# h held in SBUF through the first unit of a hybrid gMLP and Mamba-2 layer, and the gating norms' scalings moved off ScalarE

## The chip, the cores and the metric

One core of a Trainium2 chip. The metric is the device time of one execution in microseconds (us). The kernel before takes 1588.07 us, the median of three runs.

## The reference, cut to what matters

```python
def hybrid_layer(x, ...):                       # x: 2048 tokens of 1024 channels, float32
    h = rms_norm(x, pre_w)
    proj = einsum('bld,dc->blc', h, w_in)       # u, v, zg, z, xbc, dt_raw
    y_a = spatial_gating(u, v, zg, ...)
    y_b = ssd_mixer(xbc, z, dt_raw, ...)        # conv, SiLU, chunked scan, gated norm
    return x + rms_norm(concat(y_a, y_b) @ w_out, post_w)

def spatial_gating(u, v, zg, ...):
    vn = layer_norm(v, v_norm_w, v_norm_b)
    s = einsum('hts,bcshd->bcthd', tril(ws), vn) + bs    # within chunks of 128 tokens
    return grouped_rms_norm(u * s * silu(zg), out_norm_w, 128)
```

## The kernel before, in words

The tokens are four batches of 512 (b = 0 to 3), each of four chunks c of 128. The two projections run in seven **units** u: 0 and 2 make the channels xbc of two SSD groups each, 1 makes z, 3 makes v, 4 and 5 make u and zg for the gating, 6 is the output projection. A unit multiplies in Strassen-Winograd form: two pairs of batches p, (0, 2) and (1, 3), and seven products P1 to P7 over half the depth each (line 43). A **step** is one product's share of 256 in depth, `j`; a unit has 28 steps (two j), the last has 56 (four j). Each operand is split into a rounded part and its remainder (`split`, line 157: ScalarE copies, VectorE subtracts), and `mm3` (line 164, matmuls of lines 165 to 167) issues three matmuls of 128x512 for each of 2 x 4 combinations: 24 in a step. `after` (line 868) combines the products on VectorE.

The A operand of a step comes from h, the normed input, in layout [channels, tokens]. `prep(b)` (line 242) makes it: eight loads of half rows of x (256 KB each, into buffers of the `g` pool), their sums of squares on ScalarE (line 184), the inverse root on POOL, a diagonal matrix `dg` and a matmul with ones that spreads it over the partitions (`r_ps`, line 259), a copy `rb` (line 261). Then for each of four j a load of x_t (512 KB), the scaling of its two halves on VectorE (line 268), the store to the DRAM tensor `hd`, and the passes of the small dt projection on PE (line 273; the profile counts two passes for each matmul call, 64 a batch). After them comes `dt_chain` (line 286), whose cumulative sum `cs` is what the scan's decay is made from; it starts 20 time units after its batch's prep.

`make_a` (line 721) is a generator for one step: up to its `yield` it issues loads, behind it arithmetic. In unit 0 the plain products P1, P2 and P4 load one tile of `hd`, P6 loads three, P5 two, P3 one; P7 takes what P6 left. P6 subtracts twice, keeps `s3` and, by a POOL copy, `s2` for P7 and P3. Made operands of P6, P7, P5 and P3 are stored (`a_d`) and loaded by later units; unit 1 loads the plain ones from `hd` again. `look_ahead` (line 833) makes A two steps and B three steps ahead of the matmuls.

Work beside the products is in generators, too. `spawn(gen, delay)` sets one up, `yield d` asks to go on `d` time units later, and `run_tasks` lets at most a few go on after each group of six matmuls, which counts as 1.36 units (about 1 us each). `tc.issue_after` keeps what such a task puts on PE behind the matmuls already written. Stores are queued by `store` and issued 5.4 units later. All transfers are issued by SP. The framework's scheduler fixes the order on each engine from a timeline of its own, so a load that depends on nothing can be issued long before the line that asks for it.

In the gating, `spatial(b, hp)` (line 574) handles 256 channels: it loads v, normalizes it (line 584 on VectorE: minus the mean, times the weight; line 585 on ScalarE: times the inverse deviation r), multiplies with the masked matrix (line 594) and adds `SB`, the row bias (line 598, VectorE). `gate_in` (line 608) multiplies with u and SiLU(zg) when the projection's sums arrive, and `gate_out` (line 622) scales by the norm (line 627, ScalarE, eight operations of 128x128), waits 14 units and transposes (`y_tiles`, line 547). There are 16 such tiles of work in units 4 and 5; six of the eight of a unit come in its last 11 steps (`WANTED`, line 909). POOL also serves the SSD scan: lines 436, 438, 457, 464 and 465.

Buffers of a pool are shared by its tiles: `r` has 7 of 128x1024, `g` 32 of 128x515, `q` 22 of 128x256.

Of the kernel before, what the change touches and what calls it, by code (L numbers as in the profile page):

```python
# [15 lines left out]
P = 128  # L16
# [35 lines left out]
def hybrid_kernel(ctx: ExitStack, tc: tile.TileContext, x, x_t, pre_w, w_u, w_o, w_dt,  # L52
# [64 lines left out]

    def setup():
# [4 lines left out]
        nc.sync.dma_start(out=y_c[:, 8:16], in_=sn_w)  # L123
        nc.sync.dma_start(out=wsT, in_=ws_t)
# [18 lines left out]
    def row_weights(src):  # L143
        t = const.tile([P, DM], F32, name="row_w")
        nc.sync.dma_start(out=t, in_=src.partition_broadcast(P))
        return t
# [16 lines left out]

    def mm3(dst, a_hi, a_lo, b_hi, b_lo, first, last):
# [16 lines left out]
    junk = const.tile([P, WC], mybir.dt.bfloat16, name="junk")  # L181
# [53 lines left out]
    def load_x(b):  # L235
        for c in range(NT):
            for n in range(2):
                xt = gt("xt")
                nc.sync.dma_start(out=xt, in_=x[(b * NT + c) * P:(b * NT + c + 1) * P, n * WC:(n + 1) * WC])
                yield c, n, xt  # L240

    def prep(b):

        ss = sm.tile([P, NT, 2], F32, name="x_ss")
        dg = gt("dg").rearrange("p (c n) -> p c n", c=NT)
        for c, n, xt in load_x(b):
            sumsq(ss[:, c, n:n + 1], xt, WC)
        if b == 0:
            for i, v in enumerate((dt_bias, a_log, d_skip)):
                nc.sync.dma_start(out=hvec[:, i, :], in_=v.partition_broadcast(P))  # L250
            nc.scalar.activation(na, hvec[:, 1, :], AF.Exp)
            nc.vector.tensor_scalar(na, na, -1.0, None, ALU.mult)
        r = rsqrt_mean2(ss, NT, 1.0 / DM, "x")
# [9 lines left out]
        for j in range(4):  # L263
            h = rt("h")
            nc.sync.dma_start(out=h, in_=x_t[b, j])
            for kk in range(2):
                k = 2 * j + kk
                nc.vector.scalar_tensor_tensor(h[:, kk, :], h[:, kk, :], pre_c[:, k:k + 1], rb, ALU.mult, ALU.mult)
            nc.sync.dma_start(out=hd[b][j], in_=h)
            for kk in range(2):  # L270
                k = 2 * j + kk
                for c in range(NT):
                    nc.tensor.matmul(dtp[:, c * NH:(c + 1) * NH], lhsT=h[:, kk, c * P:(c + 1) * P], rhs=wdt[:, k, :],
                                     start=k == 0 and c == 0, stop=k == KT - 1 and c == NT - 1, skip_group_check=True)
            if b:
                yield 0
# [5 lines left out]
        spawn(dt_chain(b, d), 20)  # L282

# [437 lines left out]
    def make_a(u, p, name, j):  # L721
# [17 lines left out]
        if u == 0:  # L739
            yield  # L740
# [266 lines left out]
```

## Time and profile before

| | |
|---|---|
| median of three runs (lowest to highest) | 1588.07 us (1584.94 to 1588.9) |
| the profiled execution: its own time / its span | 1584.35 / 1582.6 us |
| granted TensorE clock, mean over the span | 0.979 |
| busy share of the span: PE, VectorE (DVE), ScalarE (ACT), POOL | 95%, 68%, 52%, 25% |
| moved by DMA | 494.63 MB, mean 313 GB/s |

How to read it: the span runs from the first to the last instruction of one profiled execution. PE is TensorE's matmul, PEld its weight load, SPq the sequencer that issues the transfers. A matmul's end is modelled and runs into the next one's start, so PE's busy time is more than the sum of what the matmuls need; the spacing of the starts is the better measure. A wait is put down to what came last before it ended. L12 is line 12 of the kernel.

### The profile page before, as it was taken

Reading aid. Unit: us, or ns where it says so; the run is one execution under the profiler, and the core shown is the slowest. Engines: PE = TensorE matmul, PEld = TensorE weight load, DVE = VectorE, ACT = ScalarE, POOL = GpSimd, SP = SyncE. Lnnn points to the kernel's source line nnn. Section 1 sums busy time; section 2 is a strip of 40 time slices with the busy share of each in tenths; the row PEclk is TensorE's granted clock in tenths of the full one; section 3 lists DMA queues with packets and bytes.
Section 4 is the critical chain, followed back from the end, with each engine's and each line's share of the span. In section 5 each row is a group of like instructions: output and inputs, shape, how many; then the busy total and the mean of one; then the engine's idle time right before and its main releaser. Section 6 shows DMA issues by size and latency. Waiting matters only on the chain.

```text
span 1582.6 us, 21521 instructions
## 1 busy us (share of the span) xinstructions
PE 1508.9 (95%) x7268; PEld 1258.4 (80%) x7268; DVE 1068.9 (68%) x1708; ACT 819.8 (52%) x1769; POOL 390.1 (25%) x449
## 2 busy tenths in 40 slices
PE   4979999899999999999999999989999999999996
PEld 3868887788888888888778888867888878888775
DVE  3476874678665576567786768764665646587698
ACT  4432324655676545654466666859737742333332
POOL 1000000234232333342234515353523300000022
PEclk9988999999999999999999999989999999999999
DMA  9799999999998799986998788866776598897998
GB/s 333 264 371 357 338 411 397 392 340 366 374 349 311 240 353 341 329 316 238 333 338 319 271 299 275 279 229 225 276 252 242 193 302 326 275 384 239 341 351 333
DMA packets 160847, 494.63 MB, mean 313 GB/s; under 512 B 19040, under 2 KB 35808, under 8 KB 140768
## 3 DMA queue, kind: packets, MB, share of 16 engines
q1 hardware_dynamic: 160736, 493.25, 85.9%
q8 instruction: 57, 0.93, 0.2%
q14 instruction: 54, 0.44, 0.1%
HBM read 373.51 MB, written 119.67 MB: 312 GB/s over the span
## 4 chain that ended last, share of the span: by engine, by line
PE 57%; DMA 13%; DVE 11%; ACT 7%; issue 3%; POOL 1%; SPq 1%; DVEq 0%; ACTq 0%; POOLq 0%
PE acc L165 16%; PE acc L167 16%; PE acc L166 16%; DMA E<-scr 3%; DMA r<-yd 3%; PE y_ps L448 3%; ACT E L389 2%; DMA r<-w_o 2%; PE y_ps L451 1%; PE st_ps L453 1%; DVE cv_out L372 1%; DVE a L161 1%; PE s_ps L594 1%; PE y_tp L553 1%; DVE b L161 1%
## 5 line engine op out<-in xcount | busy, mean ns | idle before, releaser
L165 PE MATMUL acc<-b,a 128*128 128x512 f32 x1344 | 544.6, 406 | 16.1 <-DMA a<-as0P 5.4
L166 PE MATMUL acc<-b,a 128*128 128x512 f32 x1344 | 527.3, 392 | 0.0
L167 PE MATMUL acc<-b,a 128*128 128x512 f32 x1344 | 520.2, 393 | 4.3 <-DVE a L161 4.3
L165 PEld LDWEIGHTS acc<-b,a 128*128 128x128 f32 x1344 | 253.7, 189 | 71.3 <-DMA a<-as0P 5.6
L167 PEld LDWEIGHTS acc<-b,a 128*128 128x128 f32 x1344 | 253.2, 188 | 60.2 <-DVE a L161 6.3
L166 PEld LDWEIGHTS acc<-b,a 128*128 128x128 f32 x1344 | 254.0, 189 | 49.3
L160 ACT ACTIVATE a<-r 128x1024 fp32r<-128x1024 f32 x96 | 101.1, 1057 | 200.8 <-PE acc L167 88.5
L165 PE MATMUL acc<-a,b 128*128 128x512 f32 x448 | 182.4, 414 | 8.3 <-ACT b L160 4.2
L372 DVE SCALAR_TENSOR_TENSOR cv_out<-cv_raw,cw,cv_out 128x512 f32<-128x512 f32 x192 | 155.1, 810 | 41.5 <-ACT cv_out L370 39.5
L161 DVE TENSOR_TENSOR b<-r,b 128x1024 fp32r<-128x1024 f32 x112 | 141.9, 1270 | 60.6 <-ACT b L160 60.4
L166 PE MATMUL acc<-a,b 128*128 128x512 f32 x448 | 180.3, 403 | 0.8 <-DVE a L161 0.8
L167 PE MATMUL acc<-a,b 128*128 128x512 f32 x448 | 177.7, 400 | 0.0
L160 ACT ACTIVATE b<-r 128x1024 fp32r<-128x1024 f32 x112 | 117.2, 1052 | 86.9 <-PE acc L167 33.1
L161 DVE TENSOR_TENSOR a<-r,a 128x1024 fp32r<-128x1024 f32 x96 | 117.3, 1223 | 50.5 <-ACT a L160 50.3
L165 PEld LDWEIGHTS acc<-a,b 128*128 128x128 f32 x448 | 87.2, 195 | 27.4 <-ACT b L160 4.3
L184 ACT ACTIVATE junk<-y 128x128 bf16<-128x128 f32 (+1 forms) x192 | 65.5, 341 | 83.1 <-POOL y L465 71.4
L457 POOL TENSOR_TENSOR state<-state,ex 128x256 f32<-128x256 f32 x60 | 46.9, 781 | 239.5 <-PE y_ps L451 239.4
L166 PEld LDWEIGHTS acc<-a,b 128*128 128x128 f32 x448 | 86.8, 194 | 19.6 <-DVE a L161 1.8
L167 PEld LDWEIGHTS acc<-a,b 128*128 128x128 f32 x448 | 86.4, 193 | 18.9 <-issue 0.2
L436 POOL TENSOR_TENSOR xde<-xtok,dte 128x256 f32<-128x256 f32 x64 | 52.3, 824 | 165.0 <-ACT xtok L408 158.7
L173 POOL TENSOR_TENSOR o_r<-o_ms,mhalf 128x1 f32<-128x1 f32 x16 | 19.0, 1198 | 295.1 <-DVE o_ms L171 285.0
L389 ACT ACTIVATE E<-E,cs 128x128 f32<-128x128 f32 x256 | 79.6, 390 | 22.2 <-DMA E<-scr 22.2
(163 smaller groups left out, 2125.8 us busy)
## 6 DMA issues: line engine op xcount, KB each, us to landing
a<-as0P SPq DMA_DIRECT2D x64, 1024.0 KB, 7.4
a<-as1P SPq DMA_DIRECT2D x64, 1024.0 KB, 6.2
r<-w_u SPq DMA_DIRECT2D x108, 512.0 KB, 6.4
r<-yd SPq DMA_DIRECT2D x72, 512.0 KB, 5.3
r<-hd SPq DMA_DIRECT2D x48, 512.0 KB, 7.5
r<-w_o SPq DMA_DIRECT2D x36, 512.0 KB, 5.2
E<-scr SPq DMA_DIRECT2D x64, 256.0 KB, 7.4
yd<-yT SPq DMA_DIRECT2D x64, 256.0 KB, 4.4
```

Source lines behind the costliest of these rows:

```text
L160: nc.scalar.activation(w[:, :, 0, :], t, AF.Copy)
L161: nc.vector.tensor_tensor(w[:, :, 1, :], t, w[:, :, 0, :], ALU.subtract)
L165: nc.tensor.matmul(dst, lhsT=a_hi, rhs=b_hi, start=first, stop=False, skip_group_check=True)
L166: nc.tensor.matmul(dst, lhsT=a_hi, rhs=b_lo, start=False, stop=False, skip_group_check=True)
L167: return nc.tensor.matmul(dst, lhsT=a_lo, rhs=b_hi, start=False, stop=last, skip_group_check=True)
L173: nc.gpsimd.tensor_tensor(r, ms, mhalf[:, 0:n], ALU.pow)
L184: nc.scalar.activation(junk[:, 0:n], src, AF.Square, accum_out=dst)
L372: nc.vector.scalar_tensor_tensor(cv, raw[:, j:j + T], cw[:, ti, j:j + 1], cv, ALU.mult, ALU.add)
L389: nc.scalar.activation(E[:, h, :], E[:, h, :], AF.Relu, scale=-1.0, bias=dts[self.b]["cs"][:, o + h:o + h + 1])
L436: nc.gpsimd.tensor_tensor(h4(xde[:, :]), xc, hv(d["dte"], g, c), ALU.mult)
L448: nc.tensor.matmul(yps[:, h * HD:(h + 1) * HD], lhsT=E[:, h, :], rhs=xdt[:, h * HD:(h + 1) * HD], start=True, stop=True)
L457: nc.gpsimd.tensor_tensor(h4(st[:, :]), h4(st[:, :]), ev(d["ex"], 1, g, c), ALU.mult)
```

## The change

- **prep** loads x as whole rows, four tiles of 512 KB in `r` buffers, and x_t as eight tiles of 256 KB in `g` buffers (`load_h`). Batches 0 and 1 issue both at once at the start; batch 2 is spawned after 2 units instead of 16, batch 3 after 10 instead of 30, and the waits between their parts are given as arguments. The sum of squares takes a whole row at a time. The scaled tiles stay in SBUF (`kept`), and are still stored to `hd`.
- **make_a in unit 0**: P1 and P2 take batch 0's and 1's tiles from `kept` (`take_h`, which runs the batch's prep on as far as needed) and split them in two halves (`split_tiles`). P6 loads one tile and takes batch 2's or 3's four from `kept`; it makes the sum for P5 there (`s1`), in four tiles of 128x256, and overwrites `a22` instead of copying it on POOL. P5 loads nothing; P3 and P4 load one tile as before.
- **look_ahead** makes the first two steps' A and B in turn.
- **held**: the loads of wsT, SB and the two row weights follow a one-column copy from batch 0's `cs`.
- **Gating**: v is normalized by one operation with two scalars; the weight is multiplied in on reading the matmul's result (VectorE), `SB` is added by POOL, and the norm's scaling is done by POOL in four operations of 128x256.

```diff
+    def held(t):
+        nc.vector.tensor_copy(t, dts[0]["cs"][:, 0:1])
...
+        held(wsT[:, 0, 0:1])
+        held(SB[:, 0, 0:1])
...
     def row_weights(src):
         t = const.tile([P, DM], F32, name="row_w")
+        held(t[:, 0:1])
         nc.sync.dma_start(out=t, in_=src.partition_broadcast(P))
         return t
...
+    def split_tiles(t):
+        w = apool.tile([P, 2, 2, T], F32R, name="a")
+        for kk in range(2):
+            n = T // len(t[kk])
+            for i, part in enumerate(t[kk]):
+                cols = slice(i * n, (i + 1) * n)
+                nc.scalar.activation(w[:, kk, 0, cols], part, AF.Copy)
+                nc.vector.tensor_tensor(w[:, kk, 1, cols], part, w[:, kk, 0, cols], ALU.subtract)
+        return w
...
+    kept, h_in = {}, set()
+    def prep(b, *waits):
+        xs = [rt("xt") for _ in range(NT)]
         for c in range(NT):
-            for n in range(2):
-                xt = gt("xt")
-                nc.sync.dma_start(out=xt, in_=x[(b * NT + c) * P:(b * NT + c + 1) * P, n * WC:(n + 1) * WC])
-                yield c, n, xt
-    def prep(b):
-        ss = sm.tile([P, NT, 2], F32, name="x_ss")
-        dg = gt("dg").rearrange("p (c n) -> p c n", c=NT)
-        for c, n, xt in load_x(b):
-            sumsq(ss[:, c, n:n + 1], xt, WC)
+            nc.sync.dma_start(out=xs[c], in_=x[(b * NT + c) * P:(b * NT + c + 1) * P, :]
+                              .rearrange("p (k t) -> p k t", k=2))
+        if b < 2:
+            hs = load_h(b)
         if b == 0:
             for i, v in enumerate((dt_bias, a_log, d_skip)):
                 nc.sync.dma_start(out=hvec[:, i, :], in_=v.partition_broadcast(P))
-            nc.scalar.activation(na, hvec[:, 1, :], AF.Exp)
-            nc.vector.tensor_scalar(na, na, -1.0, None, ALU.mult)
-        r = rsqrt_mean2(ss, NT, 1.0 / DM, "x")
+        else:
+            yield waits[0]
+        ss = sm.tile([P, NT], F32, name="x_ss")
+        for c in range(NT):
+            sumsq(ss[:, c:c + 1], xs[c][:, :, :].rearrange("p k t -> p (k t)"), DM)
+        del xs
+        r = sm.tile([P, NT], F32, name=f"x_r{b}", bufs=1)
+        nc.vector.tensor_scalar(r, ss, 1.0 / DM, EPS, ALU.mult, ALU.add)
+        nc.gpsimd.tensor_tensor(r, r, mhalf[:, 0:NT], ALU.pow)
+        if b:
+            yield waits[1]
+        if b > 1:
+            hs = load_h(b)
+            yield waits[2]
+        dg = gt("dg").rearrange("p (c n) -> p c n", c=NT)
...
-            h = rt("h")
-            nc.sync.dma_start(out=h, in_=x_t[b, j])
-            for kk in range(2):
-                k = 2 * j + kk
-                nc.vector.scalar_tensor_tensor(h[:, kk, :], h[:, kk, :], pre_c[:, k:k + 1], rb, ALU.mult, ALU.mult)
-            nc.sync.dma_start(out=hd[b][j], in_=h)
-            for kk in range(2):
-                k = 2 * j + kk
+            for k in (2 * j, 2 * j + 1):
+                nc.vector.scalar_tensor_tensor(hs[k], hs[k], pre_c[:, k:k + 1], rb, ALU.mult, ALU.mult)
+            if b < 2:
+                kept[b, j] = hs[2 * j:2 * j + 2]
+            yield 0
+            for k in (2 * j, 2 * j + 1):
+                nc.sync.dma_start(out=hd[b][j][:, k % 2, :], in_=hs[k])
+            h_in.add((b, j))
+            if b > 1:
+                kept[b, j] = hs[2 * j:2 * j + 2]
+            for k in (2 * j, 2 * j + 1):
                 for c in range(NT):
-                    nc.tensor.matmul(dtp[:, c * NH:(c + 1) * NH], lhsT=h[:, kk, c * P:(c + 1) * P], rhs=wdt[:, k, :],
+                    nc.tensor.matmul(dtp[:, c * NH:(c + 1) * NH], lhsT=hs[k][:, c * P:(c + 1) * P], rhs=wdt[:, k, :],
                                      start=k == 0 and c == 0, stop=k == KT - 1 and c == NT - 1, skip_group_check=True)
-            if b:
-                yield 0
+                hs[k] = None
+        if b == 0:
+            nc.scalar.activation(na, hvec[:, 1, :], AF.Exp)
+            nc.vector.tensor_scalar(na, na, -1.0, None, ALU.mult)
...
+    def load_h(b):
+        hs = [gt("h") for _ in range(KT)]
+        for k in range(KT):
+            nc.sync.dma_start(out=hs[k], in_=x_t[b, k // 2, :, k % 2, :])
+        return hs
+    def take_h(b, j):
+        while (b, j) not in kept:
+            advance(preps[b])
+        return kept.pop((b, j))
     dts = {}
...
-            nc.vector.scalar_tensor_tensor(vc, vc, mv[:, c, 0:1], row_w["v"][:, cols], ALU.subtract, ALU.mult)
-            nc.scalar.activation(vc, vc, AF.Copy, scale=r[:, c:c + 1])
+            nc.vector.tensor_scalar(vc, vc, mv[:, c, 0:1], r[:, c:c + 1], ALU.subtract, ALU.mult)
...
             for cc in range(2):
                 y = qt("y")
-                nc.vector.tensor_tensor(y, sps[:, cc * 256:(cc + 1) * 256],
-                                        SB[:, 2 * hp:2 * hp + 2, :].rearrange("p h d -> p (h d)"), ALU.add)
+                nc.vector.tensor_tensor(y, sps[:, cc * 256:(cc + 1) * 256], row_w["v"][:, cols], ALU.mult)
+                nc.gpsimd.tensor_tensor(y, y, SB[:, 2 * hp:2 * hp + 2, :].rearrange("p h d -> p (h d)"), ALU.add)
...
         r = rsqrt_mean(ss[:, :, :].rearrange("p c i -> p (c i)"), NT * 2, 1.0 / P, "g")
         for c in range(NT):
-            for i in range(2):
-                nc.scalar.activation(yg[c][:, i * P:(i + 1) * P], yg[c][:, i * P:(i + 1) * P], AF.Copy,
-                                     scale=r[:, 2 * c + i:2 * c + i + 1])
+            y = yg[c][:, :].rearrange("p (i d) -> p i d", i=2)
+            nc.gpsimd.tensor_tensor(y, y, r[:, 2 * c:2 * c + 2].unsqueeze(2).broadcast_to([P, 2, P]), ALU.mult)
         yield 14
         yield from y_tiles(b, yg, hp)
...
+            assert (b, 2 * k + j) in h_in
...
-    s2_in, s3_in = {}, {}
+    s1_in, s2_in, s3_in = {}, {}, {}
...
+        if u == 0 and name in ("P1", "P2"):
+            yield
+            b, k = PAIRS[p][0], PLAIN_A[name][1]
+            yield split_tiles([[h] for h in take_h(b, 2 * k + j)])
+            return
...
-        if u == 0:
-            yield
         if name == "P6":
             if u == 0:
-                t, q, r = load([piece(0, 0), piece(1, 0), piece(1, 1)])
-                tt(t, t, q, ALU.subtract)
-                s3_in[p, j] = t
-                tt(r, r, t, ALU.subtract)
-                s2 = s2_in[p, j] = [gt("s2") for _ in range(2)]
+                t, = load([piece(0, 0)])
+                yield
+                b = PAIRS[p][1]
+                a21, a22 = take_h(b, j), take_h(b, 2 + j)
+                s3_in[p, j], s2_in[p, j] = t, a22
+                s1 = s1_in[p, j] = [[], []]
                 for kk in range(2):
-                    nc.gpsimd.tensor_copy(s2[kk], r[:, kk, :])
-                t = r
+                    for cols in (slice(0, GC), slice(GC, T)):
+                        q = qt("s1")
+                        tt(q, a21[kk][:, cols], a22[kk][:, cols], ALU.add)
+                        s1[kk].append(q)
+                    tt(t[:, kk, :], t[:, kk, :], a21[kk], ALU.subtract)
+                    tt(a22[kk], a22[kk], t[:, kk, :], ALU.subtract)
+                w = split_tiles([[a] for a in a22])
+                store(a_d[p][name, j], w[:, :, :, :].bitcast(F32))
+                yield w
+                return
             else:
...
         elif name == "P7":
             if u == 0:
+                yield
                 t = s3_in.pop((p, j))
             else:
                 t, q = load([piece(0, 0), piece(1, 0)])
...
         elif name == "P5":
+            if u == 0:
+                yield
+                w = split_tiles(s1_in.pop((p, j)))
+                store(a_d[p][name, j], w[:, :, :, :].bitcast(F32))
+                yield w
+                return
             t, q = load([piece(1, 0), piece(1, 1)])
-            if u:
-                yield
+            yield
             tt(t, t, q, ALU.add)
         elif u == 0:
             t, = load([piece(0, 1)])
+            yield
             s2 = s2_in.pop((p, j))
             for kk in range(2):
                 tt(t[:, kk, :], t[:, kk, :], s2[kk], ALU.subtract)
...
         if i == 0:
             upto(0, 0, load_a)
             upto(1, 0, load_b)
+        for k in range(LOOK_A if i == 0 else 0):
+            upto(2, k, lambda *a: (load_a(*a) if looked[0] <= a[0] else None, do_a(*a),
+                                   looked.__setitem__(0, max(looked[0], a[0] + 1))))
+            upto(3, k, lambda *a: (load_b(*a) if looked[1] <= a[0] else None, do_b(*a),
+                                   looked.__setitem__(1, max(looked[1], a[0] + 1))))
...
-    spawn(prep(0))
+    preps = {0: spawn(prep(0))}
+    preps[1] = spawn(prep(1, 1, 3))
     spawn(setup())
-    spawn(prep(1), 1)
-    spawn(prep(2), 16)
-    spawn(prep(3), 30)
+    preps[2] = spawn(prep(2, 7, 0, 6), 2)
+    preps[3] = spawn(prep(3, 8, 5, 8), 10)
```

## Rows read from the trace of the kernel before

**Rows 1.** The page's part 1: busy time, share of the span, instructions.
```profile
PE 1508.9 (95%) x7268; PEld 1258.4 (80%) x7268; DVE 1068.9 (68%) x1708; ACT 819.8 (52%) x1769; POOL 390.1 (25%) x449
```

**Rows 2.** Windows by stage: busy us (instructions) of PE, PEld, DVE, ACT, POOL; granted clock; DMA.
```profile
0.00:36.90 36.90, 15.94 (x67) 14.27 (x67) 13.08 (x32) 15.57 (x38) 6.02 (x11) 1.00 0.93 326
36.90:115.20 78.30, 69.30 (x330) 57.27 (x330) 46.06 (x87) 34.67 (x63) 2.98 (x4) 0.90 0.87 317
115.20:176.80 61.60, 61.06 (x267) 51.38 (x268) 46.89 (x94) 15.03 (x23) 4.18 (x7) 0.84 0.94 359
176.80:244.60 67.80, 67.80 (x311) 56.35 (x310) 49.47 (x71) 19.84 (x21) 0.00 (x0) 1.00 0.99 383
244.60:300.60 56.00, 46.89 (x214) 37.70 (x212) 31.20 (x36) 30.11 (x47) 6.03 (x5) 0.98 1.01 390
...
970.00:1060.00 90.00, 82.27 (x426) 68.72 (x424) 66.37 (x120) 66.82 (x203) 41.74 (x46) 0.98 0.79 276
1060.00:1180.00 120.00, 115.94 (x592) 97.75 (x593) 69.69 (x125) 81.20 (x208) 45.05 (x53) 0.96 0.70 245
1180.00:1255.00 75.00, 75.00 (x392) 63.83 (x392) 47.51 (x96) 54.15 (x177) 29.63 (x34) 1.00 0.61 212
```

**Rows 3.** The same view with finer cuts, the one stretch at half clock.
```profile
116.00:131.00 15.00, 14.51 (x52) 12.83 (x52) 11.22 (x14) 3.95 (x6) 1.63 (x2) 0.50 1.02 415
```

**Rows 4.** Waits of PE from 0 to 310 us: total, times, longest.
```profile
PE r_ps L259 <- DVE dg L254: 17.9, 2, 15.2
PE acc L165 <- ACT a L160: 6.5, 3, 3.0
PE acc L165 <- DMA a<-as0P: 5.2, 1, 5.2
```

**Rows 5.** Timeline: start us, us, engine, line, operation, count [idle before].
```profile
12.19 0.63 ACT L184 ACTIVATE junk<-xt 128x512 bf16<-128x512 f32 x1
...
17.74 0.33 SPq L145 DMA_DIRECT2D row_w<-v_w  x1
...
18.85 13.83 PE L273 MATMUL dt_ps<-wdt,h 128*128 128x16 f32 x64 [1.57 <-DVE h L268]
...
28.01 0.45 SPq L153 DMA_DIRECT2D r<-w_u  x1
...
36.86 0.80 PE L165 MATMUL acc<-a,b 128*128 128x512 f32 x1 [4.18 <-ACT b L160]
...
92.55 3.64 PE L273 MATMUL dt_ps<-wdt,h 128*128 128x16 f32 x32
```

**Rows 6.** DMA of the first 244.6 us: all of it, and the reloads of h.
```profile
DMA packets 27199, 84.91 MB, mean 347 GB/s; under 512 B 4194, under 2 KB 4578, under 8 KB 25262
...
r<-hd SPq DMA_DIRECT2D x41, 512.0 KB, 7.2
```

**Rows 7.** Groups of DVE from 36.9 to 244.6 us: busy us, mean ns, idle before.
```profile
L161 DVE TENSOR_TENSOR a<-r,a 128x1024 fp32r<-128x1024 f32 x29 | 35.3, 1219 | 24.4 <-ACT a L160 24.4
...
L268 DVE SCALAR_TENSOR_TENSOR h<-h,pre_c,rb 128x512 f32<-128x512 f32 x24 | 17.0, 756 | 0.5 <-DMA h<-x_t 0.5
...
L773 DVE TENSOR_TENSOR r<-r,s 128x512 f32<-128x512 f32 x8 | 5.2, 684 | 0.0
```

**Rows 8.** Groups of the whole kernel, shapes apart: DVE, ACT and POOL in the gating.
```profile
L584 DVE SCALAR_TENSOR_TENSOR v<-v,v_mv,row_w 128x256 f32<-128x256 f32 x64 | 31.8, 539 | 15.8 <-DMA v<-vd 15.8
...
L160 ACT ACTIVATE b<-r 128x1024 fp32r<-128x1024 f32 x112 | 117.2, 1052 | 86.9 <-PE acc L167 33.1 <-DVE r L819 17.2 <-DMA r<-w_o 12.8
...
L627 ACT ACTIVATE y<-y,g_r 128x128 f32<-128x128 f32 x128 | 39.2, 392 | 18.7 <-POOL g_r L173 18.7
...
L585 ACT ACTIVATE v<-v,v_r 128x256 f32<-128x256 f32 x64 | 30.0, 501 | 21.8 <-DVE v L584 21.4
...
L616 POOL TENSOR_TENSOR y<-y,sg 128x256 f32<-128x256 f32 x64 | 54.9, 870 | 99.9 <-ACT sg L615 67.9 <-DVE c L905 10.7 <-DVE y L613 9.2
...
L457 POOL TENSOR_TENSOR state<-state,ex 128x256 f32<-128x256 f32 x60 | 46.9, 781 | 239.5 <-PE y_ps L451 239.4
```

More of the change, by code (lines that the diff above doesn't have):

```diff
@@ L179, in rsqrt_mean2 @@
         return rsqrt_mean(tot, n, inv, name)
-    junk = const.tile([P, WC], mybir.dt.bfloat16, name="junk")
+    junk = const.tile([P, DM], mybir.dt.bfloat16, name="junk")
     def sumsq(dst, src, n):
@@ L232, in flush @@
                 then()
-    def load_x(b):
+    kept, h_in = {}, set()
+    def prep(b, *waits):
+        xs = [rt("xt") for _ in range(NT)]
         for c in range(NT):
-            for n in range(2):
-                xt = gt("xt")
-                nc.sync.dma_start(out=xt, in_=x[(b * NT + c) * P:(b * NT + c + 1) * P, n * WC:(n + 1) * WC])
-                yield c, n, xt
-    def prep(b):
-        ss = sm.tile([P, NT, 2], F32, name="x_ss")
-        dg = gt("dg").rearrange("p (c n) -> p c n", c=NT)
-        for c, n, xt in load_x(b):
-            sumsq(ss[:, c, n:n + 1], xt, WC)
+            nc.sync.dma_start(out=xs[c], in_=x[(b * NT + c) * P:(b * NT + c + 1) * P, :]
+                              .rearrange("p (k t) -> p k t", k=2))
+        if b < 2:
+            hs = load_h(b)
         if b == 0:
```

## The prediction

> **What bounds the kernel now.** I read the page's totals first. PE is busy for 1508.9 of 1582.6 us while VectorE has 68% and ScalarE 52% [rows 1], so a gain has to come out of the time in which PE is held up, or works at the low clock, and of nothing else. The next view cuts the span at the unit borders and where PE falls behind [rows 2]; the reader should compare, line by line, the length of a stretch with the work in it. In 176.8 to 244.6 us PE runs twelve steps without a hole: 311 matmuls, 288 of them of the products. A small pass costs 0.114 us (32 dt passes in 3.64 us [rows 5]), so the other 23 take 2.6 us and a product matmul (67.8 - 2.6) / 288 = 0.226 us; a step of 24 is 5.44 us. Against that price the stretches before it lose: steps 0 to 7 (36.9 to 115.2) take 78.3 us for 43.5 of products and 138 x 0.114 = 15.7 of small passes, **19.1 lost**; steps 8 to 15 take 61.6 for 43.5 + 75 x 0.114 = 52.1, **9.5 lost**; the first eight steps of unit 1 (244.6 to 300.6) take 56.0 for 43.5 + 22 x 0.114 = 46.0, **10.0 lost** [rows 2]. Before all of these stand 36.9 us of startup, and in the gating units 7.7 us of idle PE in 970 to 1060 and 4.1 in 1060 to 1180.
>
> What the lost time waits for is in three views. The waits of PE [rows 4] name the first batches' norm (r_ps), splits of A, and one A load of 5.2 us. The DMA engines are at 0.94 to 1.01 from 115 us on at 359 to 390 GB/s [rows 2], so loads and stores queue there. And 116 to 131 us runs at a granted clock of 0.50, the lower level, 1.2 GHz, with VectorE busy 11.2 of 15 us [rows 3], after a stretch in which PE had been starved.
>
> **The change part by part.** Start. Now the last x sum begins at 12.19 us, the dt passes run from 18.85 for 13.8 us, the first weights are issued at 28.01 and the first product matmul starts at 36.86 [rows 5]. After: h goes from SBUF straight into the split, without a store and a reload, so what it waits for is the weights. Ahead of them SP now issues x and x_t of batch 0 and of batch 1, four times 2.1 MB, and the weights' own 0.5: 8.9 MB. At the 326 GB/s of this stretch [rows 2] that is 27.3 us, and with one ACT copy of 1.05 [rows 8] the first product starts at **28.4, 8.5 us sooner**. Bounds: at the best rate of a stretch here, 415 GB/s [rows 3], it is 22.5; from above, no sooner than now. I take the middle value since the stretch's own rate is nearest. Of the 64 dt passes of batch 0, 32 now come behind the first step: **3.6 us** given back. Three loads that were free to go early (row_w went at 17.74 [rows 5]) now wait for a one-column copy of batch 0's cs, so 1.5 MB leaves the start. On VectorE that copy stands behind the one that writes cs and holds nobody up; on SP the loads come at some 70 us, and who needs them, the row sums and the gating, comes far later: nothing. What is queued behind is another matter for x: a batch of it now takes four of the seven r buffers until ScalarE has summed it, 7 or 8 time units (about 1 us each) for batches 2 and 3, and SP's weight loads behind it wait for such a buffer. Steps 4 to 7 load no weights of their own, which is the cover; without it each late weight load would cost PE what the lookahead of three steps doesn't hold.
>
> Reloads. Of 36 loads of h in unit 0 (the view counts 41 until 244.6, five of them for unit 1 [rows 6]) 24 go: 12.6 MB of 84.9, or 36 us of DMA at 347 GB/s. The stores of h and the loads of x_t go in halves, 16 more of each, x in whole rows, 16 fewer: SP issues 8 transfers fewer in all, no matter. What this is worth is only what PE waited for. In steps 0 to 7 I take 13 of the 19.1 us away: batch 1 lies in SBUF before it is wanted and batch 2 is begun 14 time units earlier. Six stay, a first step at the slow rate as now and a wait or two. In unit 1 the DMA engines enter with less of a backlog, but steps 16 to 35 are still about as full as they can be: 67.8 us at 383 and 56.0 at 390 GB/s are 47.8 MB, less 4.2 for P5's eight reloads leaves 43.6 MB, 113 us at 386 GB/s for 20 steps whose PE floor is 113 to 114. So I take half of the 10.0, **5 us**; bounds 0 and 10.
>
> VectorE. P6 of unit 0 had three operations of 1.219 us, 3.66 together [rows 7]. It gets six of 128x512 at 0.684 and four adds of 128x256. Those are not in the trace; they lie between half of 0.684 and 0.684, I take 0.40, near the half, and have 5.70. Four tiles: **+8.2 us** within steps 6 to 15, where VectorE is busy 46.9 of 61.6 us now [rows 2] and loses about 6 more waiting for ScalarE's half of the split (24.4 us over 208 [rows 7]). Some h scaling leaves (0.756 each [rows 7]), but 46.9 + 8.2 + 6 - 5 = 56 is still over the 52.1 that PE needs, with little slack; so the 9.5 us lost there shrink by **1.5** only. P5 saves 2.44 - 1.6 us a tile, in a stretch where PE does not wait: nothing, and if that cover were gone, 3.4 us of gain. The eight POOL copies that go were beside other work: nothing.
>
> Gating units. ScalarE loses 39.2 + 30.0 = 69.2 us [rows 8]. VectorE's 64 operations of 0.539 become tensor_scalars of the same size: between none and 0.54, taken as 0.45. POOL gets 64 adds and 64 scalings of 128x256; the two like it cost 0.870 and, with a broadcast operand, 0.781 [rows 8]: up to 111 us more. In 970 to 1060, where six gating tiles fall, POOL has 41.7 of 90 us [rows 2]; with all of their 48 new operations 83.5. It fits, without much room. Queued behind them on POOL are the scan's state scaling and the gate products, which PE's transposes and y_ps need; the y_tiles call comes 14 units after the scaling and covers it. PE's 11.8 idle us there have ScalarE in the chain in part: I take **4** back; bounds -12 and +10.
>
> The sum: -8.5 + 3.6 - 13 - 1.5 - 5 - 4 = -28.4, from the profiled execution's 1584.35 (span 1582.6 and 1.75 around it) to 1556. The median of the runs shown is 3.7 above that execution, so I add 1: **1557 us**.
>
> **The rivals.** First, *VectorE takes the place of the DMA queue*: if in steps 6 to 15 the P6 work, two batches' scaling and the dt chains meet, the loss there grows from 9.5 to some 22, which gives back what steps 0 to 7 win, and only the start (-4.9) and 4 us of unit 1 remain: 1575. For it: 56 against 52 us above. Against it: lookahead lets VectorE run two steps ahead.
>
> Second, the other side: *POOL becomes the bound of the gating*. Place: the six tiles in a row near the end of units 4 and 5. POOL's 46 operations in 970 to 1060 average 0.907 us [rows 2]; with 94, it fills the 90 us from 0.957 on, and every hundredth over that costs nearly 1 us in each of two stretches. To eat the 28.4 us, the ScalarE gain included, it must reach about 1.12; at 1.2 us the stretches need 113 us, 23 lost in each, and the kernel takes 1584 - 24 + 46 = 1606. Against it: 0.870 and 0.781 are means that already hold the waits beside VectorE. The Trainium skill, GPSIMD Engine Reference, section Performance versus the Vector engine, speaks against this part of the change: it calls the engine the wrong choice for elementwise work, 1.96 times slower than VectorE in its example. By that factor on 0.539 an operation would be 1.06 us, an estimate, and 48 of them would bring the stretch to 92.6 of 90 us, some 3 us lost in each and 1567 in all; the trace's ratio, 0.870 to 0.539 or 1.6, is milder.
>
> Third, *the change does not do what it says at the start*: x and x_t of two batches ahead of the first weights only push these back, the reloads were hidden anyway, and VectorE keeps PE waiting as now: nothing gained, 3.6 given back, some us of unit 1 won: about 1584.
>
> **How the numbers follow.** Forecast 0.63, VectorE rival 0.16, POOL 0.13, no effect 0.08. Some 0.3%, 4.8 us, is what a measurement here can tell from no change. Faster: the forecast and nearly all of the first rival, 0.78. Same: the third and a rest, 0.09. Slower: POOL, 0.13. The range begins where all bounds help: start -10.8 + 3.6, losses -17 and -5, unit 1 -10, gating -12, that is 1533, rounded to 1531; it ends at 1592, which holds the first and third rival and the mild end of the second.
>
> **What would show it.** Right: the first product matmul near 28 us, 12 reloads of h in unit 0 where there were 36, step 8 near 103 us and unit 1 beginning near 225, no stretch at half clock after the start, ScalarE 69 us lighter and POOL some 105 heavier. Wrong: PE waits for VectorE's splits between 90 and 150 us; POOL over 90% near 1000 us with y_tp and y_ps waiting; the first product after 33 us.

## The result, and the profile after

The changed kernel takes 1568.45 us (median of four runs, 1561.36 to 1572.55), the kernel before 1588.49 beside it: ratio 0.9872, 95% interval 0.9847 to 0.9897, some 20 us faster. The forecast was 1557, so the sign and the range were right, and a third of the gain is missing. Executions of one kernel differ by up to some 15 us here, so comparisons of kernels go by medians, and traces, of one execution each, show where time goes. The profiled execution takes 1567.0 us with a span of 1565.2.

The page's totals, which answer to [rows 1], show less work on ScalarE (64 us) and more on POOL (94 us):

```profile
PE 1501.4 (96%) x7268; PEld 1254.1 (80%) x7268; DVE 1087.6 (69%) x1752; ACT 755.8 (48%) x1569; POOL 484.1 (31%) x569
```

The same cut by stages as in [rows 2]: startup, steps 0 to 7, 8 to 15, 16 to 27, and unit 1's first eight steps; then a stretch in the gating. Columns are PE, PEld, DVE, ACT, POOL busy with their instructions, granted clock, DMA share, GB/s:

```profile
0.00:27.00 27.00, 9.10 (x35) 7.41 (x35) 11.02 (x22) 14.72 (x26) 2.85 (x10) 1.00 0.86 319
27.00:102.00 75.00, 75.00 (x363) 64.32 (x364) 50.16 (x107) 33.23 (x58) 4.82 (x4) 0.89 0.92 343
102.00:158.70 56.70, 56.70 (x267) 48.12 (x266) 46.32 (x97) 12.57 (x19) 2.08 (x1) 0.91 0.82 316
158.70:226.50 67.80, 67.80 (x311) 56.33 (x310) 50.77 (x105) 22.07 (x36) 0.00 (x0) 1.00 0.95 348
226.50:273.80 47.30, 46.04 (x214) 37.92 (x212) 28.89 (x33) 27.33 (x40) 4.46 (x5) 1.00 1.02 398
...
949.00:1045.00 96.00, 81.27 (x417) 67.36 (x416) 76.95 (x124) 51.28 (x155) 71.20 (x83) 0.95 0.75 254
```

PE now has no idle time from its first product matmul to unit 1: 75.00 of 75.00 and 56.70 of 56.70 us. Where [rows 4] had two waits for the norm, three for splits of A and one for a load, the waits of PE in 0 to 275 us are these:

```profile
PE r_ps L287 <- DVE dg L282: 13.2, 1, 13.2
PE acc L183 <- ACT b L167: 3.2, 1, 3.2
PE dt_ps L305 <- DVE h L293: 1.6, 1, 1.6
PE acc L183 <- DMA a<-as0P: 1.3, 1, 1.3
```

What is still lost there is clock. By the prices of the prediction (24 product matmuls 5.44 us, a small pass 0.114), steps 0 to 7 need 43.5 + 171 x 0.114 = 63.0 of their 75.0 us, and 0.11 x 75.0 = 8.3 us of the 12.0 lost are the granted clock's; steps 8 to 15 need 52.1 of 56.7, and 0.09 x 56.7 = 5.1 covers all of it. (The clock column shows 1.00 at the very start, but there the product matmuls start 0.43 us apart until 31 us, against 0.23 behind it; by this spacing the first 4 us ran at the lower level too, which is 2 us more of the 12.0.) The finer windows show the clock falling to the lower level, 1.2 GHz, with PE busy throughout. The timeline has 48 dt passes in a row from 54.56 us on, and 64 in one block from 82.44 to 92.90:

```profile
55.00:60.00 5.00, 5.00 (x41) 5.00 (x40) 4.51 (x7) 2.57 (x6) 1.59 (x1) 0.87 1.05 396
60.00:65.00 5.00, 5.00 (x16) 4.13 (x16) 2.65 (x4) 2.23 (x4) 0.38 (x1) 0.50 1.05 397
...
85.00:90.00 5.00, 5.00 (x30) 5.00 (x29) 5.00 (x12) 0.00 (x0) 0.00 (x0) 0.60 0.76 283
90.00:95.00 5.00, 5.00 (x22) 4.71 (x22) 3.84 (x8) 2.00 (x2) 0.00 (x0) 0.50 0.26 107
```

The DMA of everything before unit 1 fell from the 84.91 MB of [rows 6]; loads of h went from 41 to 20 (the code asks for 12 of them in unit 0; the others are unit 1's):

```profile
DMA packets 26785, 75.82 MB, mean 335 GB/s; under 512 B 4149, under 2 KB 4533, under 8 KB 24596
...
r<-hd SPq DMA_DIRECT2D x20, 512.0 KB, 6.2
```

Then the gating. The groups with a changed place in it (line, engine, tile, count, busy us, mean ns, idle before) answer to [rows 8]:

```profile
L644 POOL TENSOR_TENSOR y<-y,SB 128x256 f32<-128x256 f32 x64 | 57.9, 923 | 37.7 <-DVE y L643 37.7
...
L672 POOL TENSOR_TENSOR y<-y,g_r 128x256 f32<-128x256 f32 x64 | 47.9, 778 | 0.7
...
L629 DVE TENSOR_SCALAR v<-v,v_mv,v_r 128x256 f32<-128x256 f32 x64 | 31.0, 521 | 17.8 <-DMA v<-vd 16.0 <-POOL g_r L191 1.8
```

The longest wait of PE behind the start lies there. The timeline, by engine (start, us, instruction, idle before it):

```profile
1027.36 2.62 POOL L191 TENSOR_TENSOR g_r<-g_ms,mhalf 128x8 f32<-128x8 f32 x1
1030.06 2.84 POOL L672 TENSOR_TENSOR y<-y,g_r 128x256 f32<-128x256 f32 x4
1032.86 0.72 POOL L509 TENSOR_TENSOR y<-y,yo 128x256 f32<-128x256 f32 x1
1033.54 0.72 POOL L644 TENSOR_TENSOR y<-y,SB 128x256 f32<-128x256 f32 x1
...
1034.30 0.93 DVE L658 TENSOR_TENSOR y<-y,u 128x256 f32<-128x256 f32 x1 [2.58 <-POOL y L644]
...
1041.56 0.41 DVE L479 TENSOR_TENSOR xdt<-xtok,dt 128x256 f32<-128x256 f32 x1
...
1042.12 1.94 PE L493 MATMUL y_ps<-xdt,E 128*128 128x64 f32 x8 [8.55 <-DVE xdt L479]
```

The root, four scalings, an add and an SB add stand in one queue. The gate's multiplication on VectorE waits 2.58 us for the last of them; convolution, v and, at its end, `xdt` stand behind it on VectorE; PE waits 8.55 us for `xdt`. Not all of this is new: the kernel before and hx_only below, which has the gating as before, wait 4.3 us there. The row of hx_only:

```profile
PE y_ps L493 <- DVE xdt L479: 4.3, 1, 4.3
```

How far each kernel is ahead of the one before, in us, read from the starts of the product matmuls of the profiled executions (24 to a step; the end is the start of the last step):

| | first product | step 8 | unit 1 | step 36 | step 104 | step 156 | end |
|---|---|---|---|---|---|---|---|
| the sum of the prediction | 8.5 | 17.9 | 19.4 | 24.4 | 24.4 | - | 28.4 |
| the change | 9.9 | 13.2 | 18.1 | 26.8 | 28.0 | 18.7 | 17.4 |
| hx_only | 10.3 | 12.4 | 22.1 | 28.9 | 31.6 | 30.2 | 30.9 |
| scale_act | 10.6 | 12.9 | 22.5 | 31.4 | 34.1 | 34.1 | 35.6 |
| no_pool | 10.5 | 12.6 | 22.3 | 31.4 | 32.8 | 31.7 | 35.0 |
| sb_dve | 8.9 | 12.1 | 18.6 | 27.3 | 28.0 | 27.4 | 29.8 |
| gate_only | -0.2 | -1.2 | -1.5 | -3.9 | -4.7 | -11.6 | -14.9 |

Each row of the table is one execution against one of the kernel before. That one (1584.35) is 4 us under its median, and gate_only's is the slowest of its ten, so its row ends at 14.9 us where the medians say 5. The change is 28.0 us ahead when the gating begins to weigh and gives 9.3 of it back between steps 104 and 156. The first of these, 3.0, go before step 114, and POOL's first new operation starts only at 818.9 us, within that step; the other 6.2 go behind it.

### The profile page after: what moved, and what is told of

The parts are those of the page before. It is cut to its first block, busy times and chain, and to the rows that moved or that the text cites. A ratio compares the mean times of both kernels' runs of the same rounds, so it can differ in the third digit from the quotient of the medians.

```text
span 1565.2 us, 21448 instructions
## 1 busy us (share of the span) xinstructions
PE 1501.4 (96%) x7268; PEld 1254.1 (80%) x7268; DVE 1087.6 (69%) x1752; ACT 755.8 (48%) x1569; POOL 484.1 (31%) x569
## 4 chain that ended last, share of the span: by engine, by line
PE 58%; DMA 15%; DVE 12%; ACT 9%; issue 3%; POOL 2%; SPq 1%; DVEq 0%; ACTq 0%; POOLq 0%
PE acc L183 16%; PE acc L185 16%; PE acc L184 16%; DMA r<-yd 3%; DMA E<-scr 3%; ACT E L434 3%; PE y_ps L493 2%; DMA r<-w_o 2%; DVE cv_out L417 2%; PE dt_ps L305 2%; DMA cv_raw<-raw 2%; DVE b L168 1%; PE y_ps L496 1%; DVE a L168 1%; PE st_ps L498 1%
## 5 line engine op out<-in xcount | busy, mean ns | idle before, releaser
L417 DVE SCALAR_TENSOR_TENSOR cv_out<-cv_raw,cw,cv_out 128x512 f32<-128x512 f32 x192 | 158.9, 830 | 31.7 <-ACT cv_out L415 28.0
L167 ACT ACTIVATE a<-r 128x1024 fp32r<-128x1024 f32 x80 | 84.5, 1057 | 160.2 <-PE acc L185 107.0
L168 DVE TENSOR_TENSOR a<-r,a 128x1024 fp32r<-128x1024 f32 x80 | 99.3, 1242 | 23.9 <-ACT a L167 23.8
L191 POOL TENSOR_TENSOR o_r<-o_ms,mhalf 128x1 f32<-128x1 f32 x16 | 18.7, 1179 | 293.6 <-DVE o_ms L189 283.5
L185 PEld LDWEIGHTS acc<-a,b 128*128 128x128 f32 x448 | 85.8, 192 | 18.7 <-issue 0.2
L184 PEld LDWEIGHTS acc<-a,b 128*128 128x128 f32 x448 | 86.3, 193 | 18.1 <-issue 0.7
L421 ACT ACTIVATE cv_out<-cv_out 128x512 f32<-128x512 f32 x64 | 40.3, 630 | 103.1 <-DVE cv_out L417 102.7
```

The costliest lines, as they stand in the source:

```text
L167: nc.scalar.activation(w[:, :, 0, :], t, AF.Copy)
L168: nc.vector.tensor_tensor(w[:, :, 1, :], t, w[:, :, 0, :], ALU.subtract)
L184: nc.tensor.matmul(dst, lhsT=a_hi, rhs=b_lo, start=False, stop=False, skip_group_check=True)
L185: return nc.tensor.matmul(dst, lhsT=a_lo, rhs=b_hi, start=False, stop=last, skip_group_check=True)
L417: nc.vector.scalar_tensor_tensor(cv, raw[:, j:j + T], cw[:, ti, j:j + 1], cv, ALU.mult, ALU.add)
L421: nc.scalar.activation(self.cv[i], self.cv[i], AF.Silu)
```

## The experiments

**The two halves apart.** hx_only takes the gating edits back, gate_only has nothing else.

```diff
hx_only:   v, SB and the norm's scaling as before; h in SBUF as in the change
gate_only: v, SB and the norm's scaling as in the change; prep and make_a as before
```

> The changed kernel with the gating as it was before: two operations for v's normalization (VectorE, ScalarE), SB added by VectorE, the norm's scaling on ScalarE. Theory (POOL): the changed kernel leads by 27 us when unit 3 ends and by 19 at the end, so the gating part costs some 8 us and this kernel keeps the 27: about 1561, ratio 0.983 to the kernel before. Rival (drift): the lead shrinks in units 4 and 5 whatever the gating does, because the SSD scan and the loads there are late in any case: 1568 to 1572, ratio 0.987 to 0.990, as the changed kernel.

> The kernel before with the gating part of the change alone. Theory (POOL): slower by some 8 us, ratio 1.005, with PE waiting for xdt and y_tp near the start of unit 5 for more than the 4.3 and 1.7 us of before, and POOL over 70% busy there. Rival (ScalarE relieved): faster by the 4 us that the prediction took, ratio 0.997. Rival (drift): no difference.

hx_only: 1554.36 us, ratio 0.9784 (0.9767 to 0.98). gate_only: 1595.29, 1.0034 (1.002 to 1.0048), with the same wait of 8.5 us of y_ps for `xdt`. So h in SBUF is worth 0.0216 x 1589 = 34 us, and the gating edits cost 5 us by themselves and 14 (0.9872 against 0.9784) together with the rest. Why more together is not shown; in the traces 3.6 of the 13.6 us between hx_only and the change are there at step 104, ahead of the gating.

**Which of the gating edits.** Three runs put POOL's two new operations back, one at a time and both.

```diff
 scale_act, no_pool:
-            nc.gpsimd.tensor_tensor(y, y, r[:, 2 * c:2 * c + 2]..., ALU.mult)
+            for i in range(2):
+                nc.scalar.activation(yg[c][:, i * P:(i + 1) * P], ..., AF.Copy, scale=r[...])
 sb_dve, no_pool:
-                nc.gpsimd.tensor_tensor(y, y, SB[...], ALU.add)
+                nc.vector.tensor_tensor(y, y, SB[...], ALU.add)
```

> The changed kernel with the norm's scaling back on ScalarE (eight operations of 128x128 a tile); v's single operation and SB on POOL stay. Theory (POOL's queue): half of the new POOL work is gone, so 2 to 5 us of the 8 come back: 1563 to 1566. Rival (ScalarE): ScalarE has 39 us more, and what its relief gave is lost: 1569 to 1572.

> The changed kernel with no new work on POOL: the norm's scaling on ScalarE as before, SB added by VectorE in an operation of its own, v's single operation kept. Theory (POOL's queue): all of the 8 us come back, and ScalarE's 30 us of relief stay: 1558 to 1561. Rival (VectorE): VectorE has 64 operations of about 0.5 us more and its order is what PE waits for: 1567 or slower.

> The changed kernel with the add of SB in the gating tiles taken back to VectorE, as an operation of its own; the norm's scaling stays on POOL. It tells POOL's total load from the place of the scaling in POOL's queue. If the scaling itself is what costs, because the scan's state scaling and the gate products stand behind it: as slow as the changed kernel, ratio 0.985 to 0.990 (1565 to 1573 us). If the sum of both operations on POOL is what costs: close to the run with the scaling back on ScalarE, ratio 0.977 to 0.981 (1553 to 1559 us).

scale_act: 1557.2 us, 0.9787 (0.9766 to 0.9808). no_pool: 1552.43, 0.9772 (0.975 to 0.9794). sb_dve: 1555.23, 0.9795 (0.9773 to 0.9817). After scale_act alone the scaling looked guilty; sb_dve keeps it on POOL and is as fast. Either operation on POOL costs nothing that these runs can tell, and the kernel with both is some 13 us slower. The traces put about half of that on the place where POOL has both: steps 114 to 155 take 334.5 us in the change and 334.9 in gate_only, which have both operations on POOL, and 327.8 to 329.9 in the kernel before and in the four versions with one or none. The rest lies ahead of POOL's first new operation or in the last unit, and its cause is open. Every edit also gives the scheduler a new order on each engine; no run holds the order fixed, so that it is POOL's load and not the order rests on both kernels with the two operations losing there, and on these rows. In two windows of 10 us at the place of the wait, POOL (the fifth busy time) is full in the changed kernel:

```profile
1020.00:1030.00 10.00, 7.42 (x32) 5.88 (x31) 7.42 (x13) 5.62 (x22) 9.99 (x11) 0.83 0.86 298
1030.00:1040.00 10.00, 3.57 (x24) 2.89 (x22) 7.42 (x11) 5.80 (x19) 9.77 (x13) 0.91 0.69 220
```

In sb_dve POOL is nearly full in the first window only, and PE (the first) works more over both:

```profile
1020.00:1030.00 10.00, 6.21 (x39) 4.85 (x37) 8.77 (x17) 4.86 (x15) 9.07 (x11) 1.00 0.81 253
1030.00:1040.00 10.00, 6.20 (x18) 4.86 (x18) 7.47 (x13) 5.35 (x20) 5.69 (x7) 0.66 0.69 237
```

Nor in scale_act:

```profile
1020.00:1030.00 10.00, 6.62 (x29) 4.72 (x29) 9.24 (x17) 6.06 (x21) 6.28 (x8) 0.87 0.85 291
1030.00:1040.00 10.00, 10.00 (x60) 8.56 (x59) 4.25 (x12) 9.83 (x27) 6.13 (x9) 1.00 0.41 131
```

ScalarE's relief itself is worth nothing measurable: hx_only, which has the old load of ScalarE, is no slower than scale_act and no_pool, or than sb_dve, which keeps the whole relief.

**Keeping h, or loading ahead?** On no_pool, P1 and P2 of the first unit reload h from DRAM; x and x_t still come ahead.

```diff
-            yield split_tiles([[h] for h in take_h(b, 2 * k + j)])
+            take_h(b, 2 * k + j)
+            t, = load([hd[b][2 * k + j]])
+            yield
+            yield split(apool, "a", t)
```

> The same version with x and x_t loaded ahead as in it, but P1 and P2 of the first unit reloading h from hd, as the kernel before did; P6 and P5 still use h from SBUF. It tells keeping h from loading ahead. If keeping h for P1 and P2 is what wins the start: the first product comes 5 to 9 us later than with it (26.4), near 33 us, what P1 and P2 of batch 1 wait for returns in part, and the time is 8 to 18 us longer, ratio 0.982 to 0.989. If loading ahead suffices: the first product moves by less than 2 us and the ratio stays at 0.977 to 0.979.

1564.34 us, 0.986 (0.9834 to 0.9885): 14 us of the 34 go, within what was expected for keeping h; but the first product comes at 40.10 us, not near 33:

```profile
40.10 0.79 PE L183 MATMUL acc<-a,b 128*128 128x512 f32 x1 [9.23 <-ACT b L167]
```

The SP queue had eight stores of h (25.43 to 31.5 us) ahead of the first reload, and the weights follow that reload, so B was late as well as A. Keeping h saves a round trip and the place of stores and loads in SP's queue.

**The three held loads.** On no_pool, without the one-column copies.

> The same version without the three one-column copies that hold back the loads of row_w, wsT and SB (1.5 MB). If what goes ahead of the first weights on the DMA queue sets the start, as the prediction had it: where these loads come ahead of the weights, the first product comes up to 1.5 MB at 326 GB/s = 4.6 us later, ratio 0.978 to 0.981. If ScalarE's sums of batch 1 set it, or the loads are issued behind the weights: the first product within 1 us of 26.4 and the ratio at 0.977.

1557.34 us, 0.981 (0.9786 to 0.9833), overlapping no_pool's interval. The first product starts 1.3 us later than in no_pool (27.7 against 26.4) and waits for the same thing, `ACT b`; SP's timeline has none of the three loads ahead of the first weights. So holding them back was not needed at the start, and the run does not test what 1.5 MB more ahead of the weights would cost.

**What brings the clock down.** On no_pool, whose clock is 1.00 for hundreds of us there, a block of extra passes ahead of step 62.

```diff
+        if i == 62:
+            dum = bank("dum")
+            for n in range(64):                      # narrow_short: 28
+                nc.tensor.matmul(dum[:, ...16 columns], lhsT=wsT[:, n % 8, :], rhs=wdt[:, n % 8, :], ...)
 wide_block: range(8), out dum, rhs SB[:, 0:4, :], 512 columns
```

> The same version with 64 more passes of 128x16 in one block ahead of a step of unit 2 (step 62 of 224, near 450 us), where the clock is 1.00 for hundreds of us; their result is not used. They are 64 x 0.114 = 7.3 us of PE. If such a block brings the clock down by itself: the profile shows a stretch at 0.50 right behind them, 7 to 14 us long, and the time grows by 7.3 plus half of that, 11 to 14 us: ratio 0.984 to 0.986. If it needs the start of the kernel: 7.3 us more, ratio 0.982, the clock stays at 1.00.

> The control to the block of narrow passes: at the same place 8 passes of 128x512 in the same type (float32), about 7 us of PE by the 0.73 us of each half in the row of r_ps or less; the result is not used. If narrow passes are the reason for the lower clock: the clock stays at 1.00 and the time grows by 6 to 8 us, ratio 0.981 to 0.983. If any pause in the product matmuls brings it down: a stretch at 0.50 as with the narrow block, 0.984 to 0.986.

> The block of narrow passes at step 62 cut from 64 to 28, which are 56 rows of the profile and 56 x 0.114 = 6.4 us, as long as the block of wide passes (6.5 us, ratio 0.9796). If it is that they are narrow: a stretch at 0.50 behind them, and some us more than the wide block, ratio 0.982 to 0.987. If the long block (128 rows, 14.6 us) fell for its length alone: the clock stays at 1.00 and the ratio is that of the wide block, 0.978 to 0.981.

narrow_block: 1583.71 us, 0.9969 (0.995 to 0.9989), 31 us more than no_pool. My price was off: a float32 matmul is two rows, so 64 are 128 x 0.114 = 14.6 us. Timeline and windows:

```profile
456.74 23.10 PE L1016 MATMUL dum<-wdt,wsT 128*128 128x16 f32 x128
```

```profile
452.00:461.00 9.00, 9.00 (x65) 8.35 (x64) 7.88 (x12) 5.11 (x11) 2.08 (x3) 1.00 0.76 290
461.00:473.00 12.00, 12.00 (x60) 12.00 (x60) 0.85 (x2) 0.63 (x1) 0.00 (x0) 0.52 0.30 110
473.00:485.00 12.00, 12.00 (x46) 10.84 (x46) 0.00 (x0) 0.00 (x0) 0.00 (x0) 0.50 0.00 0
```

The clock falls inside the block and stays down for 24 us, which costs 12: 14.6 + 12 = 26.6, and the product starts show 25.6 between steps 60 and 63; the other 5 us are not located. narrow_short: 1559.99 us, 0.9824 (0.9802 to 0.9846):

```profile
456.43 8.03 PE L1016 MATMUL dum<-wdt,wsT 128*128 128x16 f32 x56
```

```profile
455.00:461.00 6.00, 6.00 (x48) 5.71 (x47) 5.32 (x8) 2.72 (x6) 1.93 (x3) 0.98 0.63 240
461.00:467.00 6.00, 6.00 (x23) 5.43 (x23) 0.58 (x1) 0.63 (x1) 0.00 (x0) 0.50 0.57 212
```

wide_block: 1558.21 us, 0.9796 (0.9772 to 0.982), nearly as long a block, and no fall:

```profile
455.72 7.03 PE L1016 MATMUL dum<-SB,wsT 128*128 128x512 f32 x16
```

```profile
455.00:461.00 6.00, 6.00 (x17) 2.96 (x16) 5.14 (x6) 2.73 (x6) 1.40 (x2) 1.00 0.60 233
461.00:468.00 7.00, 7.00 (x33) 5.29 (x32) 0.00 (x0) 0.54 (x1) 0.00 (x0) 1.00 0.39 145
```

The intervals of the two short blocks overlap; the clock rows do not leave it open. PE is busy in all of them. The narrow block alone, far from the start and from any starved PE, is enough. The blocks differ in the columns of a pass and in the number of passes and weight loads, 56 against 16; which of the two counts was not tested.

**Spreading the dt passes.** If so, the first unit should gain by having them between the product matmuls, first in part, then all from one queue.

```diff
 dt_spread: batches 1 to 3 leave their passes to the end of prep, one k at a time
+        for k in range(KT):
+            if hs[k] is not None:
+                yield 0
+                dt_pass(k)
 dt_queue: all batches; in the step loop, after every six product matmuls
+                    if dtq:
+                        f, k = dtq.pop(0)
+                        f(k)
```

> The version with nothing of the gating norms on POOL, in which the dt passes of batches 1 to 3 no longer run in blocks of 48 and 64: the passes of a k tile (four) are issued at a time, between product matmuls, only 16 and 16 of each of batches 2 and 3 stay together. No work is added or taken away. If blocks of narrow passes are what brings the granted clock to 0.50 (6.8 us at 57 and 13.7 us at 84 in that version): both stretches vanish or shrink, unit 1 begins up to 10 us earlier, ratio 0.971 to 0.975 (1543 to 1550 us). If the clock falls there for another reason, or what is lost is VectorE's: 0.977 as before, the stretches at 0.50 still there.

> The version with nothing of the gating norms on POOL, in which every dt pass of every batch comes from one queue: the passes of one k tile (eight rows in the profile, 0.9 us) after every six product matmuls, so no block of them is left, where the first attempt at spreading left one of 40 and 16. For that P6 of the first unit writes its difference to a buffer of its own. If blocks of narrow passes bring the clock down: no stretch at 0.50 between 30 and 130 us, unit 1 begins 6 to 10 us sooner than in that version, ratio 0.971 to 0.974 (1543 to 1548 us). If the density of narrow passes over a longer stretch decides, not their coming in a block: the clock still falls somewhere in 40 to 130 us, ratio 0.976 to 0.980.

dt_spread: 1554.42 us, 0.9781 (0.9758 to 0.9804); dt_queue: 1555.02 us, 0.9795 (0.9765 to 0.9825). Neither gains. The windows say why not: over the 100 us from 35 to 135 the granted clock is 0.90 in no_pool, 0.93 in dt_spread and 0.91 in dt_queue, so 1 to 3 us of lost clock came back, less than these runs can tell.

```profile
35.00:135.00 100.00, 100.00 (x500) 86.13 (x500) 77.87 (x167) 39.23 (x69) 6.63 (x3) 0.90 0.94 356
...
35.00:135.00 100.00, 98.87 (x507) 83.61 (x507) 77.54 (x166) 38.19 (x65) 6.36 (x3) 0.93 0.95 355
...
35.00:135.00 100.00, 100.00 (x524) 85.74 (x523) 75.73 (x159) 37.55 (x64) 6.14 (x3) 0.91 0.95 356
```

In dt_queue the windows show the clock at 1.00 where eight passes come between six products (83 to 100), but low at 60 and at 115, each behind a place where the order on PE had still put 24 passes together (55.4 and 110.7 in the timeline):

```profile
60.00:65.00 5.00, 5.00 (x15) 4.03 (x15) 4.47 (x12) 1.65 (x2) 0.54 (x1) 0.50 1.04 401
...
83.00:100.00 17.00, 17.00 (x108) 15.13 (x107) 15.91 (x30) 7.42 (x11) 0.00 (x0) 1.00 0.69 229
...
115.00:120.00 5.00, 5.00 (x19) 4.42 (x19) 5.00 (x13) 0.00 (x0) 0.00 (x0) 0.50 1.02 306
```

The falls move with the passes, but I did not get rid of them. The clock fell behind 24 passes together at these two places and stayed up behind 32 at 109.40 us in no_pool; why stays open.

## Why the prediction was right, and where it was wrong

**Start: right in size, half right in reason.** 8.5 us forecast, 9.9 measured (26.99 against 36.86). The third rival, that the start gains nothing, fell with this. The step had the weights land at 27.3 us behind 8.9 MB. But SP issues x_t of batch 1 behind them, from 22.80 us on; the weights go at 16.56 and, with 7.6 to 8.2 us from issue to landing, are there at 24.2 to 24.8. What ends last is ScalarE: sums of squares of batch 1 stand ahead of the first split of B, which begins at 25.89, another 1.1 to 1.7 us.

```profile
16.56 2.73 SPq L160 DMA_DIRECT2D r<-w_u  x3
...
24.84 1.06 ACT L202 ACTIVATE junk<-xt 128x1024 bf16<-128x1024 f32 x1
...
25.89 2.94 ACT L167 ACTIVATE b<-r 128x1024 fp32r<-128x1024 f32 x3
...
26.99 0.80 PE L183 MATMUL acc<-a,b 128*128 128x512 f32 x1 [3.17 <-ACT b L167]
```

**Steps 0 to 15: the sum right, its parts not.** Forecast: 13 us of the 19.1 lost in steps 0 to 7 come back, and 1.5 of the 9.5 in steps 8 to 15. Measured: 19.1 - 12.0 = 7.1 and 9.5 - 4.6 = 4.9; together 12.0 for 14.5, and unit 1 begins at 226.5 where 225.2 was forecast; that two wrong parts nearly cancel is luck. The mark "step 8 near 103" was met (102.0), but it did not follow from the sum, which gives 115.2 - 17.9 = 97.3. The part on steps 8 to 15 read the wrong thing: it set VectorE's load against PE's need, while [rows 2] had PE busy for 61.06 of 61.60 us at a granted clock of 0.84, and 0.16 x 61.6 = 9.9 us is the whole loss. VectorE's four adds took 0.415 us, as estimated (0.40), and held nobody up (PE has no wait for VectorE's splits there); the first rival fell with that.

**"No stretch at half clock after the start": wrong.** I had put the half clock of [rows 3] down to the starved PE before it. In the changed kernel PE is not starved and the clock falls near 60, 90 and 115 us; the experiments show narrow passes to be enough. The kernel before had shown it already: [rows 3] is not its one stretch at half clock. Right behind two blocks of 32 dt passes, at 61.88 and at 92.55 us [rows 5], short falls stand in its windows, with PE busy throughout (a third such block, at 133.66, has one behind it too):

```profile
65.00:70.00 5.00, 5.00 (x18) 4.07 (x18) 1.84 (x3) 1.99 (x5) 0.00 (x0) 0.66 1.00 368
...
95.00:100.00 5.00, 5.00 (x22) 4.17 (x22) 2.90 (x11) 2.33 (x8) 0.00 (x0) 0.68 1.03 404
```

The change drew batch 1's and 2's passes together, 48 and 64 in a row where there had been 32, and its falls behind them are longer. In sum the clock still costs less than before, 8.3 + 5.1 = 13.4 us in steps 0 to 15 where it was 0.10 x 78.3 + 9.9 = 17.7. Whether the third fall comes varies among kernels with the same code there: no_pool runs steps 8 to 15 without it, at 51.90 us for a price of 52.1, and is 4 us further ahead at unit 1 than the change.

```profile
26.40:102.60 76.20, 76.20 (x364) 65.45 (x365) 51.32 (x107) 33.23 (x58) 6.09 (x4) 0.87 0.94 346
102.60:154.50 51.90, 51.90 (x267) 44.15 (x266) 44.91 (x97) 12.58 (x19) 0.82 (x1) 1.00 0.87 336
```

**Unit 1: under-sized.** 5 us forecast out of bounds of 0 and 10, 8.7 measured: 47.30 us remain against a price of 46.0. The queue had less of a backlog, as the step said, and the estimate that 20 steps of DMA need as long as PE was too pessimistic by those 3.7 us: the loads run at 348 and 398 GB/s and PE waits for one of them, 1.3 us.

**Gating units: the wrong sign.** This is the step that failed: "It fits, without much room", 4 us gained. POOL's work came out near the estimate (94 us more for 105; 0.923 and 0.778 us an operation for 0.870 and 0.781), and over 949 to 1045 us it is busy for 71.2 of 96. The step compared totals over 90 us, and the work comes in bursts: in 1020 to 1040 POOL is busy for 19.76 of 20 us, and what waits there, the gate products and the scan, feeds PE. So the second rival named the mechanism, the engine and the place, y_tp (2.6 us) and y_ps (8.6) waiting included; its point of decision (0.957 us an operation, the stretch filled) and its price (23 us a stretch) were wrong: 9.3 us are lost, 6.2 of them behind POOL's first new operation, without the stretch being filled. And its ScalarE gain was not there to be had: 64 us off an engine that PE was not waiting for bought nothing. The add of SB took POOL a median of 0.742 us in the change and VectorE 0.419 in no_pool, a factor of 1.8. The Trainium skill, GPSIMD Engine Reference, section Performance versus the Vector engine, has 1.96 in its example and advises against such work there; the runs agree with the advice only where both operations went. That the prediction's 1567 by this factor lies 1.5 us from the measured median is luck: the operations took 0.923 and 0.778 us, not 1.06.

**The total.** Between the profiled executions 1584.35 - 1567.0 = 17.4 us were gained, 28.4 was the sum. The start and unit 1 came out 1.4 and 3.7 us better, steps 0 to 15 2.5 worse, the gating 4 + 9.3 = 13.3 worse: 28.4 + 5.1 - 15.8 = 17.7. The term that decides is the gating's. One bound of the range was added up wrongly: with the first product at 22.5 us the start gains 14.4 and, less 3.6, the 10.8 of the sum, which then takes the 3.6 off once more; without that the lower end is 1530, not 1533.

**A version that beats both**: no_pool, 1552.43 us, 0.9772. scale_act, hx_only and sb_dve cannot be told from it; all four lie below the interval of the change.

## What to carry to other kernels

Work moved to an idle engine is judged in the windows where its new operations and those it already has fall together, at the length of one burst, not by a share over 90 us; and it must come off an engine that something waits for. Before a loss is given to a wait, multiply the stretch by one minus its granted clock: a busy PE can lose that way without any wait. Taking the first use's operand from SBUF saves its place in the transfer queue as well as the transfer, here 14 of 34 us.

## What the runs showed of the hardware that was not expected

The granted clock fell to the lower of its two levels (1.2 of 2.4 GHz) while PE was busy without a gap: from within a block of 56 passes of 128x16 on for some 6 us, from within 128 of them on for 24 us, and not at 16 passes of 128x512 in nearly the same time. The Trainium skill, TensorE: Matmul & The Clock Gate, section Part 1: The HAM clock gate, has the low level for an idle engine and the high one for a busy one; the rows of 461 to 485 us, 24.00 of 24.00 us busy at 0.50 to 0.52, do not agree with that. In the same rows DVE, ACT and POOL run dry and the transfers stop (110 and 0 GB/s): their waits for products and scan sums that stand behind the block on PE last 26 to 31 us.
